# Score products over all 128 rows, and compressed keys as a block diagonal, in a two-block hybrid transformer kernel

## The chip, the cores and the metric

The kernel runs on one core of one Trainium2 chip. The metric is the device time of one execution in microseconds (us). A core has a matrix engine (TensorE, PE in the profile; its weight loads are PEld), three engines for elementwise work (VectorE or DVE, ScalarE or ACT, GpSimd or POOL) and a queue that issues transfers (SP). TensorE multiplies a stationary operand of up to 128 rows by 128 columns with a moving operand of the same rows and up to 512 columns, and adds into a tile of PSUM.

## What is computed

The model has a first block of four parallel mixers with a feed-forward part, and then two layers of a second block. Each of these layers is a feed-forward part, a mixer of four groups of heads and another feed-forward part, over 512 tokens of 1024 features in float32. The change concerns the second and the third group of the mixer, four heads of 64 each:

```python
# second group (nsa): three attentions of the same queries, weighted by gates
s_c = jnp.einsum('bshd,bnd->bhsn', q, kc) * scale        # kc: 31 compressed keys, shared by the heads
p_c = masked_softmax(s_c, tok[:, -1][None, :] <= t_pos[:, None])
o_cmp = jnp.einsum('bhsn,bnd->bshd', p_c, vc)
...
o = g[:, :, 0] * o_cmp + g[:, :, 1] * o_slc + g[:, :, 2] * o_win
# third group (dsa): an index score picks 128 keys of each query, then
s = jnp.einsum('bqhd,bqkd->bhqk', qb, kg) * scale
p = masked_softmax(s, (idx <= q_pos[None, :, None])[:, None])
out = jnp.einsum('bhqk,bqkd->bqhd', p, vg)
```

With 512 tokens the eight blocks that the "selected" attention may take are all there are, and its window covers all tokens, so in the kernel both are plain causal attentions with their own keys and values.

## The kernel before, in words

Features lie on the 128 partitions and tokens on the free dimension. Every large weight is split into a high part, rounded to a format that TensorE takes at full rate (float32r), and the remainder as a low part; so are the activations, and a product is three passes (high on high, high on low, low on high; `passes`). In the trace these are the rows `mm<-ahl,whi` and `mm<-ahl,wlo`.

`mixers` runs one layer's mixer. First come the projections, the index scores of the third group, and the fourth group (`stick`) side by side with the preparation of the others: `compress` makes the compressed keys and values, `nsa` the softmax over the compressed keys. Then `attend` runs the three attentions group by group, each side by side with the output projection of a group that is already done. For each pair of heads and each of the four query tiles of 128 tokens it makes the scores of `(i + 1) * 128` keys, a softmax, and the product with the values.

`softmax_t` (line 911) is one such softmax: scores on TensorE into one of three PSUM tiles S, the maximum on VectorE (L924), the exponential on ScalarE (L356), sum and reciprocal on VectorE (L931, L932), the scaling on GpSimd (L934, L936), the transposition on TensorE (L939, one of two tiles T), a copy on ScalarE (L363), and then the products into the tile O.

The heads have 64 features, and their scores are made by `stacked` (line 402). `stack_q` puts the high and the low part of a head's queries one above the other in the 128 rows; `stack_k` holds two tiles, the high part of the keys twice and the low part of the keys twice. The first product is of all 128 rows: high and low queries on high keys. The second takes the 64 rows where the high queries lie, and the low keys. A third one, in bfloat16, adds the causal mask (`causal`) or the choice of keys (`sel`), through an identity as the stationary operand. In the trace the first two are `S<-ahl,ahl` (second group) and `S<-hz,hz` (third group; the fourth group has products of that name too, of 64 rows and 128 columns). All matmuls are issued through one helper, L370.

The compressed scores are in plain float32, which TensorE works off as two instructions a product. `compress` leaves the keys of 64 features twice, one above the other, in `kc` (128 rows, 32 columns). `nsa` multiplies, for each query tile and each of four heads, the head's 64 rows of queries by the same 64 rows of `kc`; heads of even and odd number go to two tiles S, and the mask is added from each (L1591). In the trace the products are `S<-col,hz`.

The order in each engine's queue is set when the program is built, by a scheduler that simulates the program and draws later work forward where an engine would be free. TensorE works its queue off in order. A matmul that waits for its operand or its PSUM tile holds back all that stand behind it.

Of the kernel before, what the change touches and what calls it, by code (L numbers as in the profile page):

```python
# [21 lines left out]
S = 512  # L22
# [11 lines left out]
# ---------------------------------------------------------------- host layout  # L34
# [3 lines left out]
def _blocks_t(w):  # L38
    """[K, C] -> chunks of at most RAW columns per partition: [128, blocks of 128 columns, K/128, 128], flat."""
# [7 lines left out]
def _blocks_m(w):  # L47
    """[K, C] -> per 256 columns: [128, K/128, 256], flat."""
    k, c = w.shape
    return w.reshape(k // 128, 128, c // 256, 256).transpose(2, 1, 0, 3).reshape(-1)  # L50
# [24 lines left out]
def _small(w, axis):  # L75
    """The narrow columns of the first projection on rows 0, 32, 64 and 96 of one block."""
# [13 lines left out]
# rows of a head of 64 that is turned: the two of a pair lie 16 apart, as in a head of 32  # L90
# [183 lines left out]
# ---------------------------------------------------------------- device  # L274
def turns(*gens):
    """The units of several generators in turn."""
# [21 lines left out]
class Builder:  # L298
# [17 lines left out]
    # -- small helpers  # L316
# [23 lines left out]
    def table(self, s):  # L340
        """Functions of one table set run together: what follows waits for what came before."""
# [23 lines left out]
    def add_p(self, out, a, b, op=ALU.add):  # L365
        """out = a op b on GpSimd."""
        self.nc.gpsimd.tensor_tensor(out, a, b, op)
# [13 lines left out]
    def stack_q(self, tag, z, eng):  # L381
        """Two heads of 64 rows, each as its high and low parts one above the other; the high part where the head
        lay."""
# [9 lines left out]
    def stack_k(self, tag, z, a, eng):  # L393
        """64 rows a of z: their high part twice, their low part twice."""
# [7 lines left out]
    def stacked(self, ps, q, k, h, i):  # L402
        """Scores of head h of query tile i, K = 64, at full rate (256 columns at least)."""
        w = max(256, (i + 1) * 128)
        cs, r = slice(i * 128, i * 128 + 128), slice(64 * (h % 2), 64 * (h % 2) + 64)
        self.mm(ps[:, :w], q[h][:, cs], k[0][:, :w], True, False)
        self.mm(ps[:, :w], q[h][r, cs], k[1][r, :w], False, False)

    # -- weights
    def wstream(self, name, nhalf, F, lo_pool=False, center=False, tag=None, alt=()):  # L410
        """Blocks of the weights, F columns each: a list of pieces (hi, lo). center: the mean over all columns is
        taken off each row (for all blocks in one chunk). The pieces lie in tiles of `tag` if it is given; so do the
        blocks in `alt`, in tiles of "PT"."""
# [48 lines left out]
    def cut(pieces, c=128):  # L462
        """(hi, lo) of c columns each."""
# [1233 lines left out]
```

## Time and profile before

| what | value |
|---|---|
| three runs | 3363.62, 3370.67, 3381.74 us (median 3370.67) |
| the profiled execution | span 3371.6 us from first to last instruction; no time around it is listed |
| TensorE | 3267.3 us busy (97%), 16394 matmuls |
| VectorE, ScalarE, GpSimd | 1664.1, 1248.5, 425.8 us busy (49%, 37%, 13%) |
| transfers | 275.58 MB, 82 GB/s on average |
| mean granted TensorE clock | 0.973 of full speed |

"Busy" of TensorE counts the whole duration of a matmul, from its start to the end of its results, and successive ones overlap. How fast it goes on is read from the starts: the time from one row's start to the next. [...]

### The profile page before, as it was taken

Reading aid. Unit: us, or ns where it says so; the run is one execution under the profiler, and the core shown is the slowest. Engines: PE = TensorE matmul, PEld = TensorE weight load, DVE = VectorE, ACT = ScalarE, POOL = GpSimd, SP = SyncE. Lnnn points to the kernel's source line nnn. Section 1 sums busy time; section 2 is a strip of 40 time slices with the busy share of each in tenths; the row PEclk is TensorE's granted clock in tenths of the full one; section 3 lists DMA queues with packets and bytes.
Section 4 is the critical chain, followed back from the end, with each engine's and each line's share of the span. In section 5 each row is a group of like instructions: output and inputs, shape, how many; then the busy total and the mean of one; then the engine's idle time right before and its main releaser. Section 6 shows DMA issues by size and latency. Waiting matters only on the chain.

```text
span 3371.6 us, 41243 instructions
## 1 busy us (share of the span) xinstructions
PE 3267.3 (97%) x16394; PEld 2642.9 (78%) x16398; DVE 1664.1 (49%) x2801; ACT 1248.5 (37%) x2225; POOL 425.8 (13%) x509
## 2 busy tenths in 40 slices
PE   8999999999999999999899999999999998999998
PEld 7798787888888888886567888788888764688887
DVE  4245444454333333579845333553336886453335
ACT  4354624343222222345544322332223445542223
POOL 0001001100000000231523000120004223220002
PEclk9999999999999999999879999999999897899999
DMA  3222222322222222321000222222222310012222
GB/s 134 85 75 79 78 97 85 118 88 100 97 91 100 88 96 92 113 89 53 26 26 26 100 100 89 99 76 100 88 100 76 103 45 31 14 51 100 100 91 72
DMA packets 53071, 275.58 MB, mean 82 GB/s; under 512 B 11136, under 2 KB 16144, under 8 KB 22416
## 3 DMA queue, kind: packets, MB, share of 16 engines
q1 hardware_dynamic: 52736, 272.83, 23.0%
q8 instruction: 129, 2.11, 0.3%
q14 instruction: 62, 0.51, 0.0%
q10 hardware_dynamic: 144, 0.12, 0.0%
HBM read 267.69 MB, written 2.10 MB: 80 GB/s over the span
## 4 chain that ended last, share of the span: by engine, by line
PE 87%; DVE 7%; ACT 3%; issue 1%; POOL 1%; DMA 1%; SPq 0%; ACTq 0%; DVEq 0%; POOLq 0%
PE mm L370 72%; PE S L370 6%; PE T L370 4%; PE O L370 4%; PE T L939 2%; POOL x L630 1%; DVE x L586 1%; DVE wlo L455 1%; DMA wraw<-ffn_w 1%; DVE yc L1245 1%; DVE x L620 0%; ACT L344 0%; ACT whi L363 0%; DVE gt L448 0%; DVE acc L1480 0%
## 5 line engine op out<-in xcount | busy, mean ns | idle before, releaser
L370 PE MATMUL mm<-ahl,whi 128*128 128x512 f32 (+1 forms) x5104 | 1552.1, 384 | 19.2 <-DVE ahl L634 7.6
L370 PEld LDWEIGHTS mm<-ahl,whi 128*128 128x128 f32 x5104 | 944.6, 189 | 216.5 <-issue 11.4
L363 ACT ACTIVATE whi<-wraw 128x1024 fp32r<-128x1024 f32 (+1 forms) x457 | 481.9, 1056 | 1500.7 <-PE mm L370 1406.1
L370 PE MATMUL mm<-ahl,wlo 128*128 128x512 f32 (+1 forms) x2552 | 971.9, 382 | 0.2
L455 DVE TENSOR_TENSOR wlo<-wraw,whi 128x1024 fp32r<-128x1024 f32 (+1 forms) x451 | 573.6, 1273 | 666.3 <-ACT whi L363 658.3
L370 PE MATMUL mm<-hz,whi 128*128 128x512 f32 x1792 | 560.2, 394 | 1.3 <-DVE x L1175 1.3
L370 PEld LDWEIGHTS mm<-ahl,wlo 128*128 128x128 f32 x2552 | 481.8, 189 | 94.8 <-DVE wlo L455 2.8
L370 PEld LDWEIGHTS mm<-hz,whi 128*128 128x128 f32 x1792 | 336.1, 188 | 81.2 <-DVE x L1175 3.0
L370 PE MATMUL mm<-hz,wlo 128*128 128x512 f32 x896 | 352.3, 394 | 0.0
L574 POOL TENSOR_TENSOR ss<-x,x 128x512 f32<-128x512 f32 x6 | 8.7, 1444 | 1564.5 <-DVE x L1175 1564.5
L370 PEld LDWEIGHTS mm<-hz,wlo 128*128 128x128 f32 x896 | 168.2, 188 | 39.8
L370 PE MATMUL mm<-whi,ahl 128*128 128x256 f32 x896 | 170.1, 289 | 7.2 <-DVE hz L1280 6.3
L1157 DVE SCALAR_TENSOR_TENSOR tA<-mm,tA 128x512 f32<-128x512 f32 x80 | 55.2, 690 | 242.3 <-PE mm L370 242.3
L370 PEld LDWEIGHTS mm<-whi,ahl 128*128 128x128 f32 x896 | 143.2, 194 | 11.8 <-DVE hz L1280 6.8
L370 PE MATMUL mm<-wlo,ahl 128*128 128x256 f32 x448 | 128.2, 287 | 1.5 <-DVE wlo L455 1.5
L1175 DVE TENSOR_TENSOR x<-x,mm 128x512 f32<-128x512 f32 x64 | 43.5, 685 | 140.4 <-PE mm L370 140.1
L924 DVE TENSOR_REDUCE sm<-S 128x1 f32<-128x256 f32 (+3 forms) x128 | 61.9, 487 | 97.9 <-PE S L370 91.0
L363 ACT ACTIVATE PT<-T 128x128 f32<-128x128 f32 (+3 forms) x146 | 63.4, 440 | 112.6 <-PE T L939 108.1
L370 PE MATMUL O<-PT,hz 128*64 128x128 f32 (+2 forms) x776 | 92.3, 299 | 2.2 <-ACT PT L363 2.2
L363 ACT ACTIVATE hz<-tA 128x512 fp32r<-128x512 f32 (+1 forms) x124 | 76.0, 617 | 48.3 <-DVE tA L800 40.6
L374 DVE TENSOR_TENSOR hz<-tA,hz 128x512 fp32r<-128x512 f32 (+1 forms) x124 | 82.4, 669 | 20.2 <-ACT hz L363 19.7
L370 PEld LDWEIGHTS mm<-wlo,ahl 128*128 128x128 f32 x448 | 86.9, 194 | 2.6 <-DVE wlo L455 2.1
(350 smaller groups left out, 3687.5 us busy)
## 6 DMA issues: line engine op xcount, KB each, us to landing
wraw<-ffn_w SPq DMA_DIRECT2D x132, 1024.0 KB, 4.8
wraw<-w_gate SPq DMA_DIRECT2D x16, 1024.0 KB, 4.8
wraw<-w_up SPq DMA_DIRECT2D x16, 1024.0 KB, 4.8
wraw<-w_dn SPq DMA_DIRECT2D x16, 1024.0 KB, 4.8
wraw<-w_br SPq DMA_DIRECT2D x8, 1024.0 KB, 4.8
wraw<-w_out SPq DMA_DIRECT2D x8, 1024.0 KB, 4.8
wraw<-w_o SPq DMA_DIRECT2D x4, 768.0 KB, 4.3
gt<-PT SPq DMA_DIRECT2D x48, 64.0 KB, 2.0
```

The costliest lines, as they stand in the source:

```text
L363: self.nc.scalar.activation(out, in_, AF.Copy)
L370: return self.nc.tensor.matmul(out, lhsT, rhs, start=start, stop=stop, skip_group_check=True)
L374: self.nc.vector.tensor_tensor(lo, src, hi.bitcast(F32), ALU.subtract)
L455: nc.vector.tensor_tensor(lo, r, hi.bitcast(F32), ALU.subtract)
L574: i = nc.gpsimd.tensor_tensor(s1, xs[0], xs[1], ALU.add)
L586: nc.vector.tensor_tensor(xs[d], xs[d], m0, ALU.subtract)
L630: nc.gpsimd.tensor_scalar(y, y, 1.0, be, ALU.mult, ALU.add)
L924: nc.vector.reduce_max(st[:, 0:1], ps, axis=AX.X, negate=True)
L939: nc.tensor.transpose(pt[:, j * 128:j * 128 + 128], P[:, j * 128:j * 128 + 128], self.ident)
L1157: nc.vector.scalar_tensor_tensor(s, ps, 0.5, s, ALU.mult, ALU.mult)
L1175: nc.vector.tensor_tensor(x, x, ps, ALU.add)
L1245: nc.vector.tensor_tensor(xr[r], xr[r], self.c2(f"sin{dim}")[r], ALU.mult)
```

## The change

The change has two parts. In `stacked` the second product takes all 128 rows as well: high and low queries on low keys, which adds the product of the two low parts, left out until now. Both products have the same stationary operand.

In `compress` the keys become a block diagonal of 128 rows and 64 columns: the keys in rows 0 to 63 and columns 0 to 31, again in rows 64 to 127 and columns 32 to 63, and zero elsewhere. In `nsa` one product of all 128 rows then makes the scores of two heads, both pairs go to one tile S, and one instruction adds the mask for four heads. Comments and docstrings are removed throughout.

```diff
     def stacked(self, ps, q, k, h, i):
         w = max(256, (i + 1) * 128)
-        cs, r = slice(i * 128, i * 128 + 128), slice(64 * (h % 2), 64 * (h % 2) + 64)
-        self.mm(ps[:, :w], q[h][:, cs], k[0][:, :w], True, False)
-        self.mm(ps[:, :w], q[h][r, cs], k[1][r, :w], False, False)
+        cs = slice(i * 128, i * 128 + 128)
+        for n in range(2):
+            self.mm(ps[:, :w], q[h][:, cs], k[n][:, :w], n == 0, False)
...
     def compress(self, l, cmp):
...
-        kv = self.t("col", (128, 96))
-        self.copy_a(kv, ps[:, 0:96])
-        return kv[:, 0:32], kv[:, 32:96]
+        kv = self.t("col", (128, 128))
+        nc.vector.memset(kv[:, 0:64], 0.0)
+        for s in range(2):
+            self.copy_a(kv[64 * s:64 * s + 64, 32 * s:32 * s + 32], ps[64 * s:64 * s + 64, 0:32])
+        self.copy_a(kv[:, 64:128], ps[:, 32:96])
+        return kv[:, 0:64], kv[:, 64:128]
...
     def nsa(self, l, comp, nq, nk, tok, res):
...
         for i in range(NT):
-            ps = self.p("S"), self.p("S")
+            ps = self.p("S")
             s = self.t("tA", (128, 4, 32))
             m01 = c01[:, i:i + 1].to_broadcast([128, 4, 32])
-            for e in range(2):
-                r = slice(64 * e, 64 * e + 64)
-                for h in range(2):
-                    self.mm(ps[e][:, 32 * h:32 * h + 32], nq[h][r, i * 128:i * 128 + 128], kc[r])
-                nc.vector.tensor_tensor(s[:, e:4:2], ps[e][:, 0:64].rearrange("p (h n) -> p h n", h=2),
-                                        cng[:, i:i + 1].to_broadcast([128, 2, 32]), ALU.add)
+            for h in range(2):
+                self.mm(ps[:, 64 * h:64 * h + 64], nq[h][:, i * 128:i * 128 + 128], kc)
+            nc.vector.tensor_tensor(s, ps[:, 0:128].rearrange("p (h n) -> p h n", h=4),
+                                    cng[:, i:i + 1].to_broadcast([128, 4, 32]), ALU.add)
```

The scheduler moves some of the other work with it. TensorE's queue in the compressed softmax of the first layer; a row is output, moving operand and stationary operand with the buffers' numbers, and the size of the output; `col` holds the compressed keys, `hz` the queries of two heads. Before:

```order
L370 MATMUL S_12124<-col_11431,hz_11751 128x32
L370 MATMUL S_12124<-col_11431,hz_11869 128x32
L370 MATMUL S_12155<-col_11431,hz_11751 128x32
L370 MATMUL mm_11973<-gt_11677,hz_11489 128x256
L370 MATMUL S_12155<-col_11431,hz_11869 128x32
L370 MATMUL S_12156<-col_11431,hz_11751 128x32
L370 MATMUL S_12156<-col_11431,hz_11869 128x32
```

And in the changed program:

```order
L370 MATMUL S_12122<-col_11431,hz_11872 128x64
L370 MATMUL S_12150<-col_11431,hz_11872 128x64
L370 MATMUL T_11898<-tA_11911,negones 128x384
L370 MATMUL S_12168<-col_11431,hz_11754 128x64
L370 MATMUL S_12168<-col_11431,hz_11872 128x64
L370 MATMUL mm_11976<-gt_11680,hz_11492 128x256
```

Half the products are left, each twice as wide, one tile S for each query tile instead of two.

TensorE's queue at the start of the second group's attention in the first layer, from the second pair of score products on (`S<-ahl,ahl`, then the mask); `O<-PT` are products with the values and `T<-ident` transpositions of the attention before it. Before:

```order
L370 MATMUL S_12676<-ahl_12474,ahl_12374 128x256
L370 MATMUL S_12676<-ahl_12475,ahl_12374 128x256
L370 LDWEIGHTS identb
L370 MATMUL S_12676<-negTb,identb 128x128
L370 MATMUL O_12442<-PT_12522,yc_11922 64x128
L370 MATMUL O_12442<-PT_12507,yc_11922 64x128
L370 MATMUL O_12442<-PT_12522,yc_11922 64x128
L939 MATMUL T_12568<-ident,tA_12562 128x128 x3
```

And in the changed program, where `mm<-ahl,whi` and `mm<-ahl,wlo` are products of the output projection:

```order
L370 MATMUL S_12663<-ahl_12461,ahl_12361 128x256
L370 MATMUL S_12663<-ahl_12462,ahl_12361 128x256
L370 LDWEIGHTS identb
L370 MATMUL S_12663<-negTb,identb 128x128
L370 MATMUL mm_12618<-ahl_12206,whi_12467 128x512
L370 MATMUL mm_12618<-ahl_12207,whi_12467 128x512
L370 MATMUL mm_12618<-ahl_12206,wlo_12468 128x512
L370 MATMUL mm_12618<-ahl_12208,whi_12467 128x512
L370 MATMUL mm_12618<-ahl_12209,whi_12467 128x512
L370 MATMUL mm_12618<-ahl_12208,wlo_12468 128x512
L370 MATMUL O_12429<-PT_12509,yc_11925 64x128
```

Six products of the output projection come to stand behind the second pair. The pairs themselves and the mask keep their order.

## Rows read from the trace of the kernel before

**Rows 1.** The page: span, and busy time of TensorE with its share.

```profile
span 3371.6 us, 41243 instructions
PE 3267.3 (97%) x16394; PEld 2642.9 (78%) x16398; DVE 1664.1 (49%) x2801; ACT 1248.5 (37%) x2225; POOL 425.8 (13%) x509
```

**Rows 2.** Busy time by stretch: length, engines (instructions), granted clock, DMA share, GB/s.

```profile
1677.00:1725.00 48.00, 46.33 (x160) 26.38 (x159) 19.66 (x65) 21.16 (x62) 11.95 (x18) 0.52 0.07 23
1725.00:1812.00 87.00, 84.14 (x520) 55.48 (x521) 43.00 (x133) 46.31 (x130) 20.66 (x34) 0.97 0.04 13
2842.00:2884.00 42.00, 41.03 (x140) 23.29 (x140) 15.68 (x58) 17.38 (x54) 11.79 (x17) 0.51 0.07 25
2884.00:2962.00 78.00, 76.11 (x471) 49.60 (x472) 40.55 (x123) 40.91 (x117) 17.64 (x32) 1.00 0.04 15
sum 255.00, PE 247.60 PEld 154.75 DVE 118.89 ACT 125.76 POOL 62.04; mean PE 61.90 PEld 38.69 DVE 29.72 ACT 31.44 POOL 15.51
```

**Rows 3.** The chain that ended last, 1677 to 1725 us, shares by line.

```profile
by line: PE S L370 38.0%; PE O L370 29.0%; PE T L939 18.7%; PE mm L370 10.9%; ACT whi L447 2.7%; ACT tA L356 1.4%; issue 0.1%
```

**Rows 4.** TensorE in order of time: start, us, what; pairs, each before its mask.

```profile
1744.97 0.68 PE L370 MATMUL S<-ahl,ahl 128*128 128x256 f32 x2
1745.57 0.23 PE L370 MATMUL S<-negTb,identb 128*128 128x128 bf16 x1
...
1761.86 0.93 PE L370 MATMUL S<-ahl,ahl 128*128 128x512 f32 x2
1762.72 0.23 PE L370 MATMUL S<-negTb,identb 128*128 128x128 bf16 x1
```

**Rows 5.** The same view: products that are all of 128 rows.

```profile
1835.95 0.40 PE L370 MATMUL mm<-ahl,whi 128*128 128x256 f32 x2
1836.19 0.28 PE L370 MATMUL T<-ahl,whi 128*128 128x256 f32 x1
...
1907.13 0.62 PE L370 MATMUL mm<-ahl,whi 128*128 128x512 f32 x2
1907.58 0.39 PE L370 MATMUL mm<-ahl,wlo 128*128 128x512 f32 x1
```

**Rows 6.** Score products, 1675 to 1812 us: count, ns min/median/max, first and last start, forms.

```profile
L370 PE MATMUL S<-ahl,ahl x64: 277/501/1308, 1675.4 to 1762.3; 128*128 128x256 f32 x16, 64*128 64x256 f32 x16, 128*128 128x384 f32 x8, 64*128 64x384 f32 x8
L370 PE MATMUL S<-hz,hz x32: 363/392/578, 1764.0 to 1803.7; 128*128 128x256 f32 x8, 64*128 64x256 f32 x8, 128*128 128x384 f32 x4, 64*128 64x384 f32 x4
```

**Rows 7.** A pair at the low clock; groups in 1677 to 1725 and 2842 to 2884 us.

```profile
1694.05 1.07 PE L370 MATMUL S<-ahl,ahl 128*128 128x256 f32 x2
1695.06 0.29 PE L370 MATMUL S<-negTb,identb 128*128 128x128 bf16 x1
...
L370 PE MATMUL S<-ahl,ahl 128*128 128x256 f32 (+5 forms) x30 | 19.3, 679 | 1.7 <-ACT tA L356 1.7
...
L370 PE MATMUL S<-ahl,ahl 128*128 128x256 f32 (+5 forms) x25 | 15.5, 654 | 0.0
```

**Rows 8.** Compressed scores: all products, eight in order of time, the addition of the mask.

```profile
L370 PE MATMUL S<-col,hz x64: 272/273/293, 1590.1 to 2761.7; 64*128 64x32 f32 x64
...
1601.60 0.63 PE L370 MATMUL S<-col,hz 64*128 64x32 f32 x8
1602.17 0.33 PE L370 MATMUL O<-PT,hz 128*64 128x128 f32 x2
...
L1591 DVE TENSOR_TENSOR tA<-S,c x16: 211/216/226, 1598.7 to 2762.7; 128x64 f32<-128x64 f32 x16
```

**Rows 9.** The chain that ended last, 1590 to 1640 us, shares by line.

```profile
by line: PE mm L370 13.9%; DVE yc L1245 13.0%; DVE x L586 9.2%; DVE gt L1432 6.5%; DVE sm L1601 6.3%; DVE wlo L448 5.6%; DVE yc L1243 4.6%; DVE rm L427 4.5%; DVE gt L1433 4.5%; DVE tA L1602 3.9%; PE S L370 3.8%; PE T L370 3.8%; DVE tA L1597
```

**Rows 10.** GpSimd and TensorE in order of time: scaled tiles and their transpositions.

```profile
2918.43 0.66 POOL L936 TENSOR_SCALAR tA<-tA,sm,gs 128x384 f32<-128x384 f32 x1 [0.78 <-DVE sm L932]
...
2921.56 0.50 PE L939 MATMUL T<-ident,tA 128*128 128x128 f32 x3
...
2945.81 0.44 PE L939 MATMUL T<-ident,tA 128*128 128x128 f32 x2 [0.74 <-ACT ahl L363]
```

## The prediction

> **What bounds the kernel now.** I read the totals first: TensorE is busy for 97% of the span [rows 1], so a change on it can show in the time, if the stage it is in waits for nothing else. The diff touches two stages of each of the two layers: the attention of the second and third mixer (1677 to 1812 us in the first layer, 2842 to 2962 us in the second) and the short softmax over compressed keys before it (from 1590 us).
>
> The busy time by stretch comes next [rows 2]. In the four stretches of attention, 255 us together, TensorE is busy for 247.6 us and idle for 7.4. VectorE, ScalarE and GpSimd are busy for 119, 126 and 62 us of the same 255, so each has room. [...] The chain that ends last runs over TensorE there, 38% of it the scores in S [rows 3]. So a microsecond less of TensorE in the attention is, at first, a microsecond less of the span.
>
> Busy does not mean streaming, though. A pair of score products of 256 columns takes 0.60 us at the high clock from its start to that of the mask behind it, and one of 512 columns 0.86 us [rows 4]. Products that are all of 128 rows go on at another pace: two of 256 columns in 0.24 us, two of 512 in 0.45 us [rows 5]. Between the products of a pair the engine changes from 128 rows to 64, and from 64 back to 128 at the mask; each change costs as if the product before it had to run empty.
>
> **The change part by part.**
>
> *The pairs.* In each layer there are 64 products in S from ahl and 32 from hz, thus 48 pairs: 24 of 256 columns, 12 of 384 and 12 of 512, as rows of the first layer show [rows 6]; the second is alike. After the change both products of a pair have 128 rows, as the mask has, so both changes of rows go. The instruction count stays. I price a pair afterwards by the 128-row products of rows 5: 0.24 us and 0.45 us, and 0.345 us for 384 columns, an estimate halfway between. Before, 384 columns are 0.73 us halfway between 0.60 and 0.86. At the high clock a pair thus saves 0.36, 0.385 or 0.41 us. For both layers: 48 x 0.36 = 17.3, 24 x 0.385 = 9.2, 24 x 0.41 = 9.8, together 36.3 us.
>
> At the low clock a pair of 256 columns takes 1.01 us [rows 7]; afterwards it should take twice 0.24, so 0.53 us go, 0.17 more than at the high clock. The two slow stretches hold 30 and 25 of these products [rows 7], about 27 pairs: 27 x 0.17 = 4.6 us. Together 41 us, if each stretch keeps its clock and TensorE stays the bound.
>
> *The compressed scores.* 32 products of 64 rows and 32 columns per layer, counted as instructions, become 16 of 128 rows and 64 columns. Eight of the old ones take 0.57 us until the next instruction starts, the change of rows at their end included [rows 8], so 32 cost about 2.5 to 3 us. No row shows one of 128 rows and 64 columns. From above it is bounded by the 0.12 us of one of 256 columns [rows 5], 16 x 0.12 = 1.9 us, from below by nothing much. The gain lies between 0.6 and 3 us per layer on TensorE, but from 1590 to 1640 us the chain is mostly VectorE's [rows 9], and what TensorE gains there counts only as far as it is the one waited for. Both ends for two layers: 0 and 6 us; I take 1.5, near the row of VectorE's chain.
>
> [...] The row shows eight products in 0.57 us, under 0.07 us each. [...]
>
> *VectorE and ScalarE.* Eight additions of the mask to compressed scores (0.216 us each, rows 8) go from the two layers, four per layer, at most 1.7 us, in the stretch where VectorE leads; two fillings with zero come in, no longer than that each. I take 1 us of gain, bounds -0.5 and 1.7. ScalarE writes the compressed keys with three copies where one stood. That adds perhaps 0.5 us per layer to a result which is ready long before the first product reads it; I price it at 0, and at 1 us if that lead is gone.
>
> *Order.* The order of TensorE's queue changes little in the attention; what I rest on is shown with the change: six products of the output projection now stand behind the second pair. No DMA is added or moved past another, and no wait is new; one buffer of S less is taken per query tile in the compressed softmax.
>
> *What is late next.* With TensorE earlier, the softmax of each query tile may not be ready. The depth of the queue covers that now: GpSimd has scaled a 384-column tile by 2919.09 us (2918.43 + 0.66), and TensorE transposes it at 2921.56 us [rows 10], 2.5 us later. TensorE has a pair every 2.4 us there (165 us of fast stretches over 69 pairs, worked out below); with 2.5 us of slack and a softmax of some 6 us ahead of it, my estimate, that is three or four pairs between a tile's scores and its transposition. They take off some 1.5 us; a slack of about 1 us remains. At the end of the third mixer there is none: the 256-column tile is transposed at 2945.81 us right after TensorE sat idle for 0.74 us [rows 10]. What was saved since the last full buffer is lost at such a place. The bounds are 0 and the savings of the third mixer's 32 pairs (32 x 0.38 = 12 us); I take 4 us, near the 7.4 us of idle time that exist today.
>
> *The sum.* 41 + 1.5 + 1 - 4 = 39.5 us. The profiled span is 3371.6 us; the page gives no time of its own around the span, and the three runs, 3363.62 to 3381.74 us with a median of 3370.67, lie on both sides of it, so I count nothing around it but take off the 0.9 us to the median: 3371.6 - 39.5 - 0.9 = 3331 us. With the bounds of the small terms this case reaches from 3318 to 3342.
>
> **The rivals.**
>
> *The clock comes back sooner.* In the slow stretches the engine is held by changes of rows; without them, the same columns come in less time, and six dense products now stand behind the second pair. The slow stretches would last 48 - 15 x 0.53 = 40 us and 42 - 12.5 x 0.53 = 35 us; if half of that ran at the high clock, some 18 us more would go: 3313 us, and 3294 if all of it did. For it: the clock does come back at 1725 and 2884 us, where such products are mixed in [rows 2]. Against it: it falls just after 1677 us, where TensorE waits 1.7 us (48.00 - 46.33), and nothing in the change takes that away. [...]
>
> *The softmax becomes the bound.* If each of the 96 pairs is followed by a wait of 0.2 us for ScalarE or GpSimd, half of the gain goes back: 41 - 19 - 1.5, about 3350 us. For it: the missing slack at the end of the third mixer. Against it: 1 us of slack elsewhere, and the other engines at half load.
>
> *It doesn't do what it says.* The cost may lie not in the change of rows but in that both products and the mask add into one tile of S. Then only the small terms stay, about 3368 us. Against it: the 512-column products of rows 5 are also added up in one tile, at 0.227 us each.
>
> *Slower: the fast half of the attention turns slow.* TensorE, now ahead of the softmax, waits as it does at 1677 us, and the clock falls there too. The fast stretches are 87 + 78 us with 69 of the pairs; less 69 x 0.38 = 26 us that leaves 139 us. A pair at the low clock costs 1.01 / 0.60 = 1.7 times as much, so all of it at that level would add 97 us: 3428 us. It outweighs the gain from 57 of these 139 us on. Against it: these stretches hold the dense products of the output projection and idle for 4.7 us of 165.
>
> **How the numbers follow.** My forecast 52%; the clock back sooner 27%; the softmax as bound 12%; no effect 5%; slower 4%. A measurement of this kernel can tell about 0.5%, 17 us, from no change, so "faster" ends at 3353.8 us. Forecast and clock case are faster, and of the softmax case (3342 to 3358) some 7 of 12: 86%. The rest of it and no effect are the same: 10%. Slower 4%. The range from 3302 to 3353 leaves out no effect, slower, a part of the softmax case and the deepest clock case, together some 18%.
>
> **What would show it.** Right: a pair of 256 columns takes about 0.24 us to the mask at the high clock and one of 512 about 0.45; the count of 64-row products in S from ahl and hz falls to those of the fourth mixer; the stretches of attention get shorter by some 20 us each, with the idle time up by only a few. The clock case would show in slow stretches much shorter than 40 and 35 us. Wrong: pairs that still take 0.6 us, or TensorE idle for more than 20 us in the attention behind ScalarE or GpSimd.

## The result and the profile after

The changed kernel takes 3313.93 us (median of four runs, 3313.87 to 3320.39); beside it the kernel before took 3367.14 us (four runs, 3360.69 to 3381.74). The ratio is 0.9849, 95% interval 0.9828 to 0.9871. The forecast was 3331 us with a range of 3302 to 3353: the time lies in the range, 17 us below the forecast, where the rival "the clock comes back sooner" had put it.

The page of the changed kernel, totals; the mean granted clock of this run is 0.984, that of the profiled run of before 0.973:

```profile
span 3312.1 us, 41186 instructions
PE 3206.3 (97%) x16366; PEld 2622.8 (79%) x16366; DVE 1660.5 (50%) x2795; ACT 1245.8 (38%) x2229; POOL 426.7 (13%) x509
```

The four stretches of attention, columns as in [rows 2]:

```profile
1677.00:1691.00 14.00, 11.95 (x73) 8.42 (x71) 12.88 (x35) 11.43 (x31) 5.60 (x7) 0.88 0.02 4
1691.00:1785.00 94.00, 90.85 (x622) 63.55 (x620) 53.03 (x170) 58.01 (x169) 28.79 (x47) 0.98 0.07 23
2802.00:2816.00 14.00, 14.00 (x104) 9.98 (x102) 13.76 (x43) 13.02 (x40) 6.74 (x10) 1.00 0.00 1
2816.00:2907.00 91.00, 88.13 (x587) 60.92 (x585) 50.74 (x161) 54.49 (x157) 28.66 (x44) 0.98 0.07 24
sum 213.00, PE 204.93 PEld 142.87 DVE 130.41 ACT 136.95 POOL 69.80; mean PE 51.23 PEld 35.72 DVE 32.60 ACT 34.24 POOL 17.45
```

In the clock records of this trace and of that of before only two values stand, 0.5 and 1.0 of full speed: the low and the high clock; a value between is a mean over both. Where [rows 2] had 48 and 42 us at 0.52 and 0.51, nothing of that length is left: the clock is 0.88 in the first 14 us and 0.98 or more after that. [Rows 2] come from a run below the usual clock of the kernel before, which is 0.977 (next section), so a part of this difference is one between runs. TensorE's idle time is 8.07 us (213.00 - 204.93), 7.40 before. So the attention got shorter without waiting more.

TensorE in order of time at the high clock, pairs behind a transposition, behind products with values, and behind dense products (columns as in [rows 4]):

```profile
1692.42 0.33 PE L939 MATMUL T<-ident,tA 128*128 128x128 f32 x1
1692.50 0.48 PE L370 MATMUL S<-ahl,ahl 128*128 128x256 f32 x2
1692.83 0.23 PE L370 MATMUL S<-negTb,identb 128*128 128x128 bf16 x1
...
1700.95 0.65 PE L370 MATMUL O<-PT,hz 128*64 128x128 f32 x6
1701.53 0.73 PE L370 MATMUL S<-ahl,ahl 128*128 128x512 f32 x2
1702.11 0.23 PE L370 MATMUL S<-negTb,identb 128*128 128x128 bf16 x1
...
1708.22 0.40 PE L370 MATMUL mm<-ahl,whi 128*128 128x512 f32 x1
1708.46 0.62 PE L370 MATMUL S<-ahl,ahl 128*128 128x512 f32 x2
1708.92 0.23 PE L370 MATMUL S<-negTb,identb 128*128 128x128 bf16 x1
```

Read from start to start: a pair of 256 columns takes 0.33 us to its mask, not 0.24; one of 512 takes 0.58 us behind products with values, and 0.46 us, as predicted, only behind dense products of its own kind.

The score products of the first layer, which answer to [rows 6], and the compressed scores, which answer to [rows 8]. The second block is the kernel before, its compressed scores in the first layer alone, for their first and last start:

```profile
L370 PE MATMUL S<-ahl,ahl x64: 274/365/582, 1679.2 to 1741.0; 128*128 128x256 f32 x32, 128*128 128x384 f32 x16, 128*128 128x512 f32 x16
L370 PE MATMUL S<-hz,hz x32: 275/364/585, 1742.6 to 1777.8; 128*128 128x256 f32 x16, 128*128 128x384 f32 x8, 128*128 128x512 f32 x8
L370 PE MATMUL S<-col,hz x16: 218/275/323, 1595.7 to 1605.8; 128*128 128x64 f32 x16
```

```profile
L370 PE MATMUL S<-col,hz x32: 272/273/293, 1590.1 to 1603.5; 64*128 64x32 f32 x32
```

No 64-row product is left in the pairs, and the compressed scores go from their first product to their last in 10.1 us instead of 13.4 (10.0 and 13.5 us in the second layer). Other work lies between these products.

What TensorE waited for in 1679 to 1785 us (total, times, longest):

```profile
PE T L939 <- POOL tA L934: 2.7, 3, 1.7
PE O L370 <- ACT PT L363: 1.4, 4, 0.6
PE T L939 <- ACT PT L363: 1.1, 2, 0.6
```

The wait of 1.7 us at the start of the attention is still there. After it the clock falls, as it did before, but comes back after some 3 us (0.88 over the 14 us from 1677 is 3.4 us at the low clock).

### The profile page after: what moved, and what is told of

The parts are those of the page before. It is cut to its first block, busy times and chain, and to the rows that moved or that the text cites. A ratio compares the mean times of both kernels' runs of the same rounds, so it can differ in the third digit from the quotient of the medians.

```text
span 3312.1 us, 41186 instructions
## 1 busy us (share of the span) xinstructions
PE 3206.3 (97%) x16366; PEld 2622.8 (79%) x16366; DVE 1660.5 (50%) x2795; ACT 1245.8 (38%) x2229; POOL 426.7 (13%) x509
## 4 chain that ended last, share of the span: by engine, by line
PE 87%; DVE 6%; ACT 3%; POOL 1%; DMA 1%; issue 1%; SPq 0%; ACTq 0%; POOLq 0%; DVEq 0%
PE mm L370 73%; PE S L370 5%; PE T L370 4%; PE O L370 3%; PE T L939 1%; DVE wlo L455 1%; POOL x L630 1%; DVE x L586 1%; DMA wraw<-ffn_w 1%; ACT whi L363 1%; DVE yc L1245 1%; DVE x L620 0%; ACT L344 0%; DVE yc L1243 0%; DVE gt L448 0%
## 5 line engine op out<-in xcount | busy, mean ns | idle before, releaser
L363 ACT ACTIVATE PT<-T 128x128 f32<-128x128 f32 (+3 forms) x146 | 63.8, 442 | 67.3 <-PE T L939 62.7
```

Source lines behind the costliest of these rows:

```text
L363: self.nc.scalar.activation(out, in_, AF.Copy)
```

## The experiments

A word on the clock first, since most verdicts rest on it: runs of one and the same kernel differ in it. Beside the experiments the kernel before ran 72 times, between 3341.85 and 3380.41 us, and the time follows the mean granted clock of the run: 26 runs at 0.977 lie at 3362.3 to 3365.3 us, six at 0.984 at 3342.7 to 3348.3. That is 2.7 us for 0.001, and the rounding of the clock to three places alone is worth 1.3 us. So I compare kernels in two ways, by their medians and at an equal clock of 0.984, which takes the clock's part out. Few runs lie at just 0.984, so the last column carries every run of a kernel to it by 2.7 us for 0.001 and sets the mean against the same mean of the 72 runs of before (3345.2):

| kernel | median us | usual clock | us at 0.984 | against before at 0.984 | all runs, carried |
|---|---|---|---|---|---|
| before | 3361 to 3364 | 0.977 | 3345.1 (6 runs) | | |
| third group's pairs alone | 3357.28 | 0.970 to 0.984 | 3335.9 (1 run) | -9.2 | -9.2 |
| all pairs alone | 3322.01 | 0.983 | 3317.8 (1 run) | -27.3 | -27.1 |
| compressed scores alone | 3336.16 | 0.985 | 3339.2 (1 run) | -5.9 | -4.5 |
| after | 3313.93 | 0.984 | 3313.9 (3 runs) | -31.2 | -30.3 |
| after + tiny product, 128 rows | 3330.30 | 0.983 | 3330.2 (1 run) | -14.9 | -17.0 |
| after + tiny product, 64 rows | 3348.82 | 0.982 | 3346.1 (halfway between 0.983 and 0.985) | +1.0 | -0.2 |
| before + first product twice | 3356.01 | 0.983 | 3356.7 (2 runs) | +11.6 | +8.9 |
| before + mask head by head | 3347.81 | 0.976 to 0.985 | 3339.6 (1 run) | -5.5 | -3.6 |
| before + three copies for one | 3361.74 | 0.972 to 0.984 | 3345.6 (3 runs) | +0.5 | +0.1 |

One row warns: the mask head by head adds work on VectorE and takes none off TensorE, and yet it is 4 to 5 us faster at an equal clock. So a difference of this size at an equal clock can be the scheduler's other order, and need not be the edit itself.

### The pairs alone

`stacked` as in the change, everything else as before:

```diff
-        self.mm(ps[:, :w], q[h][:, cs], k[0][:, :w], True, False)
-        self.mm(ps[:, :w], q[h][r, cs], k[1][r, :w], False, False)
+        for n in range(2):
+            self.mm(ps[:, :w], q[h][:, cs], k[n][:, :w], n == 0, False)
```

> The kernel before with the pairs alone changed (both products of 128 rows); the compressed scores stay as they were. Theory: every change between products of 128 and of 64 rows makes TensorE run empty, and the low clock in the first half of each attention follows from these changes; then nearly the whole gain is here, 48 to 56 us, a time of 3311 to 3319 us, and both attentions run at a granted clock above 0.9. Rival, the order (dense products drawn forward with the compressed part) brought the clock back: the clock stays near 0.5 in the first 40 us of each attention, and the gain is 27 to 35 us, 3332 to 3340 us.

Measured: 3322.01 us (3317.75 to 3324.27), ratio 0.9879 (0.9866 to 0.9892), 41 us less than before; between the two expectations. At an equal clock it is 27.3 us. The order of TensorE's queue in the first layer's attention is that of before, without the six dense products, and still the clock is back; the stretches 1691 to 1725 and 2842 to 2884 us:

```profile
1691.00:1725.00 34.00, 34.00 (x225) 23.43 (x224) 19.63 (x63) 20.40 (x60) 10.75 (x17) 1.00 0.17 62
2842.00:2884.00 42.00, 42.00 (x305) 29.01 (x303) 23.16 (x81) 26.69 (x79) 12.31 (x22) 1.00 0.07 27
```

The rival fails in its sharp form: the drawn-forward products are not needed. Nor are they enough. In the second layer the kernel before already has six such products behind the second pair, shortly before this stretch, and all the same its clock is low in it (0.51 in [rows 2]):

```profile
2838.18 0.70 PE L370 MATMUL mm<-ahl,whi 128*128 128x512 f32 x2
2838.73 0.40 PE L370 MATMUL mm<-ahl,wlo 128*128 128x512 f32 x1
2838.96 0.62 PE L370 MATMUL mm<-ahl,whi 128*128 128x512 f32 x2
2839.42 0.40 PE L370 MATMUL mm<-ahl,wlo 128*128 128x512 f32 x1
...
2842.97 1.11 PE L939 MATMUL T<-ident,tA 128*128 128x128 f32 x4 [1.46 <-POOL tA L934]
2843.73 1.07 PE L370 MATMUL S<-ahl,ahl 128*128 128x256 f32 x2
```

### The changes of rows put back, and a control

Into the kernel after, between the two products of a pair, a product of zeros with 64 rows, or with all 128:

```diff
+            if n == 0:
+                self.mm(ps[:, 0:32], self.identb[r], self.negT[r, 0:1].to_broadcast([r.stop - r.start, 32]), False, False)
```

`r` is `slice(64, 128)` in the first and `slice(0, 128)` in the second.

> The kernel after, with one tiny product of 64 rows and 32 columns of zeros (bfloat16) between the two products of each pair: nothing is added to the scores, but the two changes of rows of each pair are back, while both long products keep 128 rows. Theory: TensorE runs empty at the changes as before, and the clock is low again at the start of each attention; the time goes back to 3355 to 3375 us. Rival, it was the 128 rows of the second product or the order that helped: 96 products of 0.03 to 0.1 us add 3 to 10 us to the 3314 us of after, 3317 to 3324 us, and the clock stays high.

> The control: the kernel after with the same tiny product of zeros in the same place, of 128 rows instead of 64, so that no change of rows comes in. Both theories: 96 products of 0.03 to 0.1 us, 3317 to 3324 us, clock as in after. If this one is as slow as the one with 64 rows, an extra product between the two is what costs, not the change of rows.

Measured: 3348.82 us (3343.40 to 3352.28) and 3330.30 us (3324.72 to 3332.94). A pair of 384 columns with each, at the high clock, both behind a transposition:

```profile
1700.70 0.42 PE L370 MATMUL S<-ahl,ahl 128*128 128x384 f32 x1
1701.05 0.19 PE L370 MATMUL S<-negTb,identb 64*128 64x32 bf16 x1
1701.17 0.44 PE L370 MATMUL S<-ahl,ahl 128*128 128x384 f32 x1
1701.45 0.23 PE L370 MATMUL S<-negTb,identb 128*128 128x128 bf16 x1
```

```profile
1698.42 0.42 PE L370 MATMUL S<-ahl,ahl 128*128 128x384 f32 x1
1698.68 0.19 PE L370 MATMUL S<-negTb,identb 128*128 128x32 bf16 x1
1698.72 0.42 PE L370 MATMUL S<-ahl,ahl 128*128 128x384 f32 x1
1698.99 0.23 PE L370 MATMUL S<-negTb,identb 128*128 128x128 bf16 x1
```

From the pair's start to the mask it is 0.75 us with 64 rows and 0.57 with 128; the medians of all pairs behind a transposition differ by 0.19 us at 256, 384 and 512 columns alike. So the two changes around the tiny product cost 0.19 us, and over 96 pairs 18 us; 16 to 17 us lie between the two kernels at an equal clock. The control itself cost more than expected, 0.13 us a pair (0.57 against 0.44 without it). With both, the pair is near its old 0.72 us and the kernel at its old time at an equal clock. Some 40 to 50% of that way back is the extra product, so its time alone would prove little; what speaks for the changes of rows is the difference between the two runs.

But the other half of my expectation failed: the clock did not go back to where it was. In this run it never fell at the wait in the first layer (1.00 from 1677 to 1725 us). In the second layer it fell and came back after some 7 us, with the changes of rows in place:

```profile
2829.00:2843.00 14.00, 14.00 (x85) 10.07 (x85) 8.38 (x34) 9.89 (x33) 4.02 (x8) 0.76 0.12 38
2843.00:2870.00 27.00, 27.00 (x159) 16.87 (x157) 14.10 (x42) 14.52 (x38) 8.17 (x12) 1.00 0.06 22
```

### The third group's pairs alone

```diff
-                self.stacked(ps, qs, k, h, i)
+                self.stacked(ps, qs, k, h, i, True)
```

`True` asks for a second product of 128 rows; the second group stays as before.

> The kernel before with the pairs of the third group alone changed. All of its 32 pairs stood at the high clock before. Theory with the size as the trace of after shows it (0.26 to 0.30 us a pair): 9 us less, 3358 us. With the size that was predicted (0.36 to 0.41 us): 12 us less, 3355 us. The low-clock stretches of the second group stay at about 0.5 in both. If the order or something outside the second group carries the gain, 20 us or more less, under 3347 us.

Measured: 3357.28 us, twelve runs from 3335.87 (clock 0.984) to 3374.42 us (0.970); ratio 0.9988 (0.9965 to 1.0010), which does not tell it from no change. At an equal clock it is 9.2 us, 0.29 us a pair, the size that the trace of after shows and not the predicted one. The second group is untouched, and yet in the profiled run its low stretch of the first layer has shrunk to some 10 us (0.76 and 0.95 where before had 0.57 and 0.50). In the second layer it is as long as before:

```profile
2828.00:2868.00 40.00, 40.00 (x138) 22.54 (x138) 14.50 (x54) 16.18 (x49) 10.19 (x15) 0.50 0.08 27
```

So 64-row pairs do not hold the clock down every time, but in one and the same run they can do both.

### The compressed scores alone

`compress` and `nsa` as in the change, the pairs as before.

> The kernel before with the compressed keys as a block diagonal alone; the pairs stay of 128 and 64 rows. What the first four runs leave open is why the clock stays low at the start of each attention: the tiny products of 64 rows brought the changes back and the clock stayed high. Theory: it is the 64-row pairs themselves (longer with less in them), so here the clock is as low as before and the gain is 0 to 6 us, 3357 to 3363 us at a mean granted clock of 0.977. Rival: the compressed part and the order that comes with it carry the clock; then it is 0.982 or more and the time 3340 to 3345 us.

Measured: 3336.16 us (3329.47 to 3355.64), ratio 0.9935 (0.9917 to 0.9954). My theory fails and the clock is the rival's: 25 us, of which 4.5 to 5.9 are left at an equal clock. The pairs have 64 rows as before, and the clock is back, in the same two stretches:

```profile
1691.00:1725.00 34.00, 34.00 (x189) 21.17 (x187) 15.89 (x58) 18.34 (x53) 12.00 (x18) 0.95 0.09 32
2842.00:2884.00 42.00, 42.00 (x252) 26.47 (x252) 21.75 (x68) 21.24 (x60) 11.39 (x18) 1.00 0.07 27
```

### More dense work beside the 64-row pairs

```diff
-        self.mm(ps[:, :w], q[h][:, cs], k[0][:, :w], True, False)
+        for _ in range(2 if twice else 1):
+            self.mm(ps[:, :w], q[h][:, cs], k[0][:, :w], True, False)
```

`twice` is set for the second group only.

> The kernel before with more work: the first product of each pair of the second group (all 128 rows) is issued twice, the second one overwriting the first. Both changes of rows and the 64-row product stay. The 64 extra products cost 32 x 0.12 + 16 x 0.175 + 16 x 0.23 = 10 us at the high clock and up to 20 us at the low one. Theory, the clock comes back when TensorE's time holds enough dense products: the clock rises to 0.982 or more, 19 us come back, and the time is 3352 to 3356 us in spite of the added work. Rival, the 64-row products keep the clock low whatever stands beside them: 0.975 to 0.978 and 3373 to 3383 us.

Measured: 3356.01 us (3350.08 to 3366.60), clock 0.983, ratio 0.9988 (0.9971 to 1.0005). With some 10 us more to do (9 to 12 us at an equal clock) it is not shown to be slower or faster; the clock has made up for the work, as the theory said. It proves less than I thought, since the scheduler's order came out quite different as well.

### Edits that change none of TensorE's work

The addition of the mask to the compressed scores head by head (first), and three copies on ScalarE for one (second):

```diff
+                for h in range(2):
+                    nc.vector.tensor_tensor(s[:, e + 2 * h], ps[e][:, 32 * h:32 * h + 32], cng[:, i], ALU.add)
```

> The kernel before, with nothing changed on TensorE: the addition of the mask to the compressed scores is written head by head, eight more small instructions on VectorE in each layer (8 x 0.2 us, at most 3 us more for both layers). The scheduler's order comes out otherwise for it: six dense products stand behind the second pair of the second group in both layers, as they do in the kernel with the block diagonal alone. Theory: the part of the gain that is clock comes from the order and from when the waits fall, and no edit of the scores is needed for it; then the mean granted clock is 0.982 or more and the time 3335 to 3350 us, though there is more to do. Rival: it is the block diagonal's own; then 0.977 to 0.979 and 3361 to 3367 us.

> The kernel before with the compressed keys and values copied by three instructions on ScalarE where one stood, as in the change, but into the same layout; all of TensorE's queue is in the same order as before. Theory (order decides, with some chance): 0.976 to 0.979 and 3358 to 3365 us, as before. Rival (a shift of a fraction of a microsecond is enough): the clock moves too, to 0.982 or more, and the time to 3340 to 3350 us.

Measured: 3347.81 us (twelve runs, 3339.60 to 3363.91; ratio 0.9963, 0.9936 to 0.9990) and 3361.74 us (twelve runs, 3345.10 to 3375.19; ratio 0.9992, 0.9966 to 1.0018). The first has only more to do. Its order is another, at the start of both attentions the one of the compressed scores alone, and the median falls by 16 us: 11 to 13 us of clock, which lies between 0.976 and 0.985, and the rest at an equal clock, perhaps by the order. The second has TensorE's queue of before and its time. But in its profiled run, at a mean of 0.984, the same queue is low in the first layer for some 10 us only, where [rows 2] show 48, and not at all where they show 42:

```profile
1677.00:1691.00 14.00, 12.31 (x51) 7.48 (x49) 12.35 (x30) 12.86 (x33) 7.94 (x8) 0.76 0.00 1
1691.00:1725.00 34.00, 34.00 (x198) 21.41 (x198) 16.63 (x57) 17.64 (x54) 10.37 (x17) 0.95 0.09 32
2842.00:2884.00 42.00, 42.00 (x246) 26.52 (x245) 22.28 (x66) 21.42 (x60) 11.60 (x18) 1.00 0.08 26
```

So whether the clock falls, and how long it stays low, differs from run to run with one queue; by the medians, how often seems to depend on the order.

### The unit of the attention by itself

What holds the low clock, apart from order and chance? Stretches of dense products, a wait, and 24 equal units. In a first attempt the scheduler drew the products with values and the transpositions to the front, so that the units were not the ones written, and nothing is read from its 687 us; its expectation was:

> Not the model: a stretch by itself, twelve times: 88 dense products of 512 columns, a wait of about 1, 2 and 3 us, and then 24 times the same unit as in the attention (pair of 256 columns, mask, two products with values, three transpositions). Four kinds of unit: as before (128 and 64 rows), as after (both 128), as after with the tiny 64-row product of zeros, and as before with the first product twice. Price: a pair as before 0.60 us to the mask at the high clock, as after 0.33 to 0.35, with the zeros 0.5 to 0.6. Theory (density): after a wait that lowers the clock it stays at 0.5 through most or all of the 60 us of units as before, and comes back within 10 to 15 us for the other three kinds. Rival (the clock depends on waits alone): it comes back equally soon for all four kinds.

With the order fixed by dependencies, four kinds of unit, six stretches each; the unit in short:

```python
mm(ps, q, k0)                       # 256 columns; "twice": issued twice
if kind == "zero64": mm(ps[:, 0:32], identb[64:128], zeros)
mm(ps, q[r], k1[r])                 # r: 64 rows in "before" and "twice", else 128
mm(ps[:, 0:128], identb, negT)      # mask; then two products with values, three transpositions
```

> Not the model: 24 stretches, each of 80 to 102 dense products of 512 columns, a wait, and 24 times one unit (a pair of 256 columns, mask, two products with values, three transpositions), with TensorE's order now fixed by dependencies, which the first attempt lacked. Kinds of unit in turn: as before, as after, as after with the tiny product of 64 rows, as before with the first product twice. Price from a pair's start to its mask, at the high clock behind a transposition: as before 0.60, as after 0.35, with the tiny product 0.55 us. Theory (64-row pairs hold the low clock longer): in stretches where the wait lowers the clock it returns after 5 to 10 us for full pairs and after more than 20 us, or not at all in 24 units, for pairs as before. Rival (chance alone): the spread of the return is the same for all kinds.

> Not the model: 24 stretches as in the run before (dense products, a wait, 24 units in fixed order). What is left is whether the clock is held low by the changes of rows or by the rows that a product leaves unused, or by an extra product. Kinds in turn: as before (128 and 64 rows); both of 128 rows with the tiny product of zeros of 128 rows between them; second product of 96 rows (in the traces products of 96 rows follow those of 128 without a delay); all three of the pair of 96 rows. Theory, the changes: as before stays at the low clock in at least 4 of 6 stretches for all 24 units; the three other kinds return within 10 us in all 18 stretches, at about 1.2 us a unit. Rival, unused rows: the kinds of 96 rows stay low too, the one of three 96-row products more often. Rival, the extra instruction: the kind with the tiny product stays low as the one with 64 rows did.

Stretches of 24 units in the first of the two, in turn as before, as after, with the tiny 64-row product, and with the first product twice:

```profile
307.20:364.00 56.80, 56.76 (x241) 35.80 (x242) 0.00 (x0) 0.00 (x0) 0.00 (x0) 0.51 0.00 1
690.20:720.00 29.80, 29.74 (x242) 22.54 (x243) 0.00 (x0) 0.01 (x1) 0.00 (x0) 0.94 0.00 1
439.90:497.90 58.00, 57.98 (x265) 39.26 (x266) 0.00 (x0) 0.00 (x0) 0.00 (x0) 0.52 0.00 1
519.20:581.20 62.00, 61.92 (x263) 40.88 (x264) 0.00 (x0) 0.03 (x1) 0.00 (x0) 0.51 0.00 1
```

And in the second: as before, the tiny product with 128 rows, second product of 96 rows, all three of 96:

```profile
274.70:331.30 56.60, 56.55 (x239) 35.56 (x240) 0.00 (x0) 0.00 (x0) 0.00 (x0) 0.51 0.00 1
1092.40:1130.80 38.40, 38.34 (x266) 28.44 (x267) 0.00 (x0) 0.01 (x1) 0.00 (x0) 0.78 0.00 1
1154.70:1185.30 30.60, 30.54 (x242) 22.88 (x243) 0.00 (x0) 0.01 (x1) 0.00 (x0) 0.91 0.00 1
222.90:254.00 31.10, 31.05 (x242) 23.44 (x243) 0.00 (x0) 0.00 (x0) 0.00 (x0) 0.89 0.00 1
```

In each row TensorE is busy throughout; what differs is the granted clock, and with it the length. Over all stretches:

| unit | stretches | clock fell in | of these low for all 24 units | granted clock where it fell | length us where it fell |
|---|---|---|---|---|---|
| as before, 128 and 64 rows | 12 | 11 | 11 | 0.50 to 0.52 | 56.0 to 57.5 |
| tiny product of 64 rows | 6 | 6 | 6 | 0.50 to 0.52 | 57.5 to 58.8 |
| as before, first product twice | 6 | 6 | 6 | 0.50 to 0.52 | 61.2 to 62.7 |
| as after, 128 rows | 6 | 4 | 0 | 0.89 to 0.94 | 29.2 to 30.5 |
| second product of 96 rows | 6 | 4 | 0 | 0.89 to 0.94 | 29.3 to 30.7 |
| all three of 96 rows | 6 | 5 | 0 | 0.84 to 0.94 | 29.2 to 32.1 |
| tiny product of 128 rows | 6 | 5 | 0 | 0.74 to 0.90 | 33.7 to 39.6 |

The prices hold: at the high clock a pair takes 0.61 us as before and 0.33 us as after. And this is the clearest answer of the study on the clock. In this unit each kind with a change between 128 and 64 rows inside the pair kept the low clock in all 23 stretches in which it fell; each kind without one got the high clock back in all 18, those of 96 rows as fast as the full ones. So it is not the rows left unused. That it is the change, and not a product of 64 rows as such, is likely but not shown, for no kind had 64-row products without a change. The tiny product of 128 rows takes longer to return, up to some 20 us against 10, so an extra small instruction works in the same direction; here my expectation of 10 us for all three kinds was missed. More dense products in the unit do not help while the change stays, against what I concluded from the run with the first product twice.

### The rule carried on to the fourth group

The fourth group's 64-row score products filled up to 128 rows: each head's queries in a tile of their own, zero in the other head's rows.

```diff
-                        self.mm(z[...], k[pr][r, j * 128:j * 128 + 128], q[pr][r, cs], j == 0, False)
+                        self.mm(z[...], k[pr][:, j * 128:j * 128 + 128], q[2 * pr + s][:, cs], j == 0, False)
```

> The kernel after, and the rule carried on to the fourth group: the queries of each of its heads lie in a tile of their own with zeros in the other head's rows, so its score products have 128 rows as well; four more fillings with zero on GpSimd and two more copies on ScalarE per layer. The changes of tile size in TensorE's program fall from 428 to 382. Theory: 46 x 0.1 us at the high clock, 5 us less than after where TensorE is the bound, 3305 to 3314 us and a ratio to before of 0.981 to 0.985, if the clock stays at 0.984. Rival: in that stretch VectorE leads, or the new copies delay it; 3314 to 3322 us.

Measured: 3303.81 us (five runs, 3302.78 to 3304.64), below every run of after; ratio to before 0.9826 (0.9805 to 0.9846). Its clock is 0.987; 0.003 more is 8 us by the slope above, so of the 10 us some 2 are less work, where 5 were expected, and the rest is clock. The intervals of the two ratios overlap and the two kernels did not run side by side, so that it beats after is likely, not shown.

## Why the prediction was right, and where its sum was not

The 53 us between the medians part into 22 us of clock (3367.1 to 3345.1, the four runs of before and before at 0.984) and 31 us at an equal clock (3345.1 to 3313.9). By the medians of all the runs of before, 3361 to 3364 us, the clock's part is 16 to 19 us.

The case that the forecast of 3331 us stood for, with a reach from 3318 to 3342, did not come. Its saving of 39.5 us was 31 at an equal clock, so at the clock of before the time would have been some 3336 us; the rest is the clock, for which the range, but not that case, had left room.

*The bound.* Right: what TensorE saved in the attention came out of the span, and its idle time rose by 0.7 us only.

*The pairs, 36.3 us.* The mechanism was right: a tiny product of 64 rows between the two brings back 0.19 us a pair that the same product of 128 rows does not. The size was off. The step that failed is "I price a pair afterwards by the 128-row products of rows 5: 0.24 us and 0.45 us". Those products follow others of their own kind. A pair mostly follows a transposition, a mask or products with values, and its first product then goes on some 0.1 us later, as it did before the change. Of 92 pairs whose three instructions stand together in the trace of after, ten follow dense products and take 0.24, 0.36 and 0.46 us; behind transpositions the medians are 0.324, 0.440 and 0.550, before they were 0.606, 0.721 and 0.839. The saving is 0.282, 0.281 and 0.289 us; over 48, 24 and 24 pairs that makes 27 us, and the pairs alone measure 27. Behind dense products it is the same: 0.522 before and 0.240 after, for 256 columns. The price before had the late start in it and the price after had not.

Of these 0.28 us some 0.09 lie before the 64-row product and 0.19 behind it, at each of the three widths, so it is no slower rate of columns. Behind a tiny 64-row product the way back costs 0.10 us instead of 0.19; why the wide one costs more is not shown.

The prediction has each change cost "as if the product before it had to run empty". What the trace of before shows is this: in the 89 of its 96 pairs whose three instructions stand together, at all three widths and at both clocks, the product behind a change of rows starts 0.07 us before the end of the one before it, while products of 128 rows that follow each other start 0.16 us before it, as in [rows 5]; in the trace of after the products of a pair start 0.16 us before it too. The profile models these ends, so more about the mechanism is not shown. The price these runs show at the high clock is 0.19 us for two changes around a tiny product and 0.28 us around a wide one.

*The low stretches, 4.6 us.* The condition "if each stretch keeps its clock" was the wrong case: no stretch kept it. The rival I had at 27% came true in its time. Its reason, "held by changes of rows", is borne out by the stretch of units; in the kernel itself it is not shown, for there the clock also came back with the changes in place. Two parts of its argument did not hold. The six dense products behind the second pair are not needed (the pairs alone lack them in the first layer), and new they are in the first layer only: before had them in the second, at the low clock. And I wrote against it that the wait at 1677 us would stay: it stays, the clock falls, and then comes back. That the rival's 3313 us and the measured 3313.9 agree is partly luck: it had 41 + 18 us in it where the runs show 31 at an equal clock and 22 of clock.

A busy TensorE alone did not bring the high clock back: in the first row of the units it was busy for 56.76 of 56.80 us, and the granted clock was 0.51.

*The compressed scores and VectorE, 2.5 us.* Perhaps undersized: 4.5 to 5.9 us at an equal clock. But the mask head by head, which has 64-row products as before, is 3.6 to 5.5 us faster as well, so the equal clock does not say how much is the block diagonal's own. The traces say a little more. In four of them the granted clock from 1410 to 1675 us is the same, 0.92; there the attention of the first layer begins at 1679.2 (after) and 1679.8 us (compressed scores alone) with the block diagonal, at 1681.0 (third group alone) and 1681.7 us (mask head by head) without it. That is 1.2 to 2.5 us in this layer, and 2 to 5 us for two, an estimate, where I took 2.5. On TensorE the block diagonal was no loss here: for one query tile, eight old instructions took 0.57 us [rows 8], and four new ones take 0.39 us (1604.39 to 1604.78):

```profile
1604.39 0.55 PE L370 MATMUL S<-col,hz 128*128 128x64 f32 x4
1604.78 0.86 PE L370 MATMUL T<-tA,negones 128*128 128x384 f32 x2
```

*New waits, -4 us.* Oversized: 0.7 us more idle time. *The softmax as bound* and *slower* did not come; the waits on GpSimd and ScalarE in the first layer's attention are 5.2 us in all. *It doesn't do what it says* is ruled out by the pair of 384 columns that took 0.75, 0.57 and 0.44 us behind a transposition, with the same sum in one tile of S.

What stays open: how the 22 us of clock divide between the changes of rows and the order. In the kernel, the pairs alone, the compressed scores alone and an edit that leaves TensorE's work as it is brought 14, 19 and 11 us of it by median (to 0.984), so it is there once and not to be added up. The units by themselves say that the changes of rows, or the 64-row products, can hold the low clock (0.50 to 0.52 in all 23 stretches in which it fell); the kernel before leaves it early in some runs, and why it does is not shown.

## What to carry to other kernels

Fill up the rows of a product that stands between full ones, if its operands allow it: here each filled-up pair became 0.28 us cheaper at the high clock. A change between 128 and 64 rows cost time of its own here, 0.19 us for two of them around a tiny product, and after a wait it went with a low clock (0.50 to 0.52) for as long as such products lasted in 23 stretches of the units, and for 48 us in one run of the kernel. Price an operation by rows with the same neighbours in front, on both sides of the subtraction. And before a gain of half a per cent is put down to an edit, compare at an equal granted clock: here an edit that only added work "gained" 16 us. Even then 4 to 5 us of that stayed, so a few microseconds can be the scheduler's order.

## What was not expected of the hardware

With one and the same queue, the low clock at the start of the attention lasted 48 us in one profiled run and some 10 us in another (before, and the copies alone), and in the second layer 42 us and none; the first run was 28 us longer. A wait of some 1.5 us after 19 to 25 us of dense products was followed by a fall in 11 of 16 stretches of units. And a product behind one of another kind goes on late even where both have 128 rows: a pair of 256 columns takes 0.33 us behind a transposition and 0.24 us behind dense products.
